# Gate and up products of a gated FFN: three partial sums kept in one PSUM bank, three VectorE additions a call in place of seven

## Chip, cores and metric
The kernel runs on one core of one Trainium2 chip. The metric is the device time of one execution in microseconds (us); lower is better. The chip multiplies on TensorE (PE), adds elementwise on VectorE (DVE) and GpSimd (POOL), applies functions and copies on ScalarE (ACT), and starts most transfers from SyncE (SP).

## What is computed
The reference is a two-layer decoder trunk on 1024 tokens of width 1024 in float32: layer 0 mixes tokens by a convolution module, layer 1 by stick-breaking attention. Both layers then do the part that the change is in:

```python
u = x @ w_up                                        # (1024, 1024) @ (1024, 2816)
g = causal_dwconv(x @ w_gate, conv_w, conv_b)       # 3 taps along the tokens
ffn = (silu(g) * u) @ w_down                        # (1024, 2816) @ (2816, 1024)
x = layer_norm(ALPHA * x + ffn + ple, ln_g, ln_b)
```

## The kernel before
Every float32 operand of a product is split into a high and a low part, and a product is three matmuls (high by high, high by low, low by high), lines 137 to 139 in `mm3`. High parts are cast on ACT, low parts are a subtraction on POOL or DVE (line 86).

`ffn_phase` (line 235) runs once in each layer. It takes the 2816 columns in steps of two tiles of 128 (`f` = 0, 2, ..., 20). A step calls `gate`, then `down` for the two tiles of the step before, then `up`. `gate` and `up` each call `fast` (line 311), so there are 11 steps by 2 calls by 2 layers, 44 calls.

A call of `fast` does a two by two block product (two halves of the contracted width, two column tiles, two halves of the tokens) by seven block products in place of eight (Winograd's form of Strassen's method). `fast_w` (line 286) loads the weights, forms their sums on DVE (line 294) and splits seven blocks on ACT (line 299) and POOL. A block product `prod(j, ps, x)` is 12 matmuls of 128x512 into one PSUM bank. The sums of the products are formed by `add` (line 322) on DVE, which reads one operand from a bank and the other from a `pt` tile in SBUF; `p1` is first copied there by ACT (line 326).

`fast` gets four banks `pa, pb, pc, pd`. There are two sets of four, used in turn by `gate`, `down` and `up`:

```python
(b0, b2), (b1, b3) = ((t[:, 0:HALF], t[:, HALF:]) for t in (big(), big()))
quads = turns(([b0, b1, b2, b3], banks))
```

So in one set `pa` and `pc` are the two halves of one tile of 1024 columns, `big0`, and `pb` and `pd` those of another, `big1`; a profile row names both `big`. In the other set each bank is a tile of its own, `bank`. By the turns, 24 of the 44 calls work in `big`: in each layer `gate` at f = 0, `gate` and `up` at f = 2, 6, 10, 14 and 18, and `up` at f = 20. The other 20 work in `bank`. `down` (line 374) works in the set that the `gate` before it did not use: it adds the product of the hidden tiles and `w_down` to the residual, 16 groups of six matmuls, each followed by an addition on DVE (line 383).

After `fast`, `gate` reads the four banks with ACT (line 348) and DVE (line 353), `up` with DVE (line 364), then ACT casts (line 366) and DVE subtracts (line 86) to get the parts of the hidden tile `f` that `down` reads.

Nothing is ordered by hand here. The library that builds the program sets the order of the instructions on each engine from their order in the source and from its own estimate of when each is ready, so matmuls of `down` and of the next call stand between the products of a call. It also places all waits.

Of the kernel before, what the change touches and what calls it, by code (L numbers as in the profile page):

```python
# [15 lines left out]
DRAM = bass.MemoryType.DRAM  # L16
# [5 lines left out]
HALF = 512  # L22
# [29 lines left out]
def trunk_kernel(ctx: ExitStack, tc, x, p, a_pw1_w, a_pw1_b, a_dw_w, a_dw_b, a_ln_g, a_ln_b, a_pw2_w, a_pw2_b,  # L52
# [37 lines left out]

    # ---------------------------------------------------------------- constants
    # one tile for all of them
    ctile = const.tile([P, 352], F32, name="ctile")
# [17 lines left out]
    class Rows:  # L111
        """Tiles of 4 KB, three to a slot."""

# [22 lines left out]
    def mm3(o, sh, sl, mh, ml, first, last):  # L136
        nc.tensor.matmul(out=o, lhsT=sh, rhs=mh, start=first, stop=False)  # L137
        nc.tensor.matmul(out=o, lhsT=sh, rhs=ml, start=False, stop=False)  # L138
        nc.tensor.matmul(out=o, lhsT=sl, rhs=mh, start=False, stop=last)  # L139

    def new_half():
        """High and low parts of a matrix (k, t) for the tokens of a half, in two tiles of four k blocks each."""
        return [[xtp.tile([P, 4, HALF], F32R, name="xT", align_bytes=A4) for _ in range(2)] for _ in range(2)]
# [20 lines left out]
    def ln_stats(src):  # L164
        nt = np_.tile([P, 24], F32, name="norm")
        st, mv, ve = nt[:, 0:12].rearrange("p (i s) -> p i s", i=2), nt[:, 12:14], nt[:, 14:16]
        rstd, tmp, nb = nt[:, 16:17], nt[:, 17:18], nt[:, 18:19]
        for i in range(2):
            nc.vector.bn_stats(out=st[:, i, :], in_=src[:, i * HALF:(i + 1) * HALF])
        nc.vector.bn_aggr(out=mv, in_=st)  # L170
        # reciprocal square root: a first guess from the exponent bits, then Newton steps to float32
        nc.vector.tensor_scalar(out=ve[:, 0:1], in0=mv[:, 1:2], scalar1=EPS, scalar2=None, op0=ALU.add)
        nc.vector.tensor_scalar(out=ve[:, 1:2], in0=mv[:, 1:2], scalar1=EPS, scalar2=-0.5, op0=ALU.add, op1=ALU.mult)
        nc.vector.tensor_scalar(out=tmp.bitcast(I32), in0=ve[:, 0:1].bitcast(I32), scalar1=1, scalar2=None,
                                op0=ALU.logical_shift_right)
        nc.vector.tensor_scalar(out=rstd.bitcast(I32), in0=tmp.bitcast(I32), scalar1=-1.0, scalar2=float(0x5f3759df),
                                op0=ALU.mult, op1=ALU.add)
        for _ in range(3):
            nc.vector.scalar_tensor_tensor(out=tmp, in0=rstd, scalar=ve[:, 1:2], in1=rstd, op0=ALU.mult, op1=ALU.mult)
            nc.vector.scalar_tensor_tensor(out=rstd, in0=tmp, scalar=1.5, in1=rstd, op0=ALU.add, op1=ALU.mult)  # L180
        return mv, rstd, nb
# [11 lines left out]

    # ---------------------------------------------------------------- p @ ple_w_proj, kept in DRAM until it is needed
    def ple_proj(i, sb, dst):
        """Pieces of work that need no result of the trunk."""
        pT, ws = [], []
# [36 lines left out]

    # ---------------------------------------------------------------- conv gated FFN + per-layer embedding
    def ffn_phase(i, xT, res, pp, g, b, sb, finish):
# [35 lines left out]

        # Gate and up projection: (W11 W21; W12 W22) of the two k halves and two column tiles, times (x11 x12; x21 x22) of
        # the two k halves and token halves, in seven block products (Strassen's, in Winograd's form).
        (x11, x21), (x12, x22) = ([[part[b] for part in xT[half]] for b in range(2)] for half in range(2))
# [10 lines left out]
        def fast_w(w, f):  # L286
# [9 lines left out]
            def split(full):  # L296
                hl = wslot(F32R).rearrange("p (o k n) -> p o k n", o=2, k=4)
                h, l = hl[:, 0], hl[:, 1]
                nc.scalar.copy(out=h, in_=full)  # L299
                sub_l(nc.gpsimd, l, full, h)  # L300
                return h, l
# [4 lines left out]
            add(s2, s1, a11, ALU.subtract)  # L306
            ws = [split(t) for t in (a11, s2, s1, a21, a12)]
            add(a12, a12, s2, ALU.subtract)
            return ws + [split(a12), split(a22)]

        def fast(w, f, quad):
            """The products of column tiles f and f + 1 with all tokens, each in two parts."""
            pa, pb, pc, pd = quad
            ws = fast_w(w, f)

            def prod(j, ps, x):
                (wh, wl), (xh, xl) = ws[j], x
                for k in range(4):
                    mm3(ps, wh[:, k, :], wl[:, k, :], xh[:, k, :], xl[:, k, :], k == 0, k == 3)

            def add(out, ps, t):
                nc.vector.tensor_tensor(out=out, in0=ps, in1=t, op=ALU.add)

            p1, u2 = parts()
            prod(0, pa, x11)
            nc.scalar.copy(out=p1, in_=pa)
            prod(1, pb, t2)
            add(u2, pb, p1)
            u5, u7 = parts()
            prod(2, pc, t1)  # L330
            add(u5, pc, u2)
            prod(3, pd, t3)
            add(u7, pd, u2)
            add(pd, pd, u5)
            prod(4, pa, x21)
            add(pa, pa, p1)
            prod(5, pb, x22)
            add(pb, pb, u5)
            prod(6, pc, t4)
            add(pc, pc, u7)  # L340
            return [[(pa, 0), (pb, HALF)], [(pc, 0), (pd, HALF)]]

# [41 lines left out]

        # two sets of four banks
        (b0, b2), (b1, b3) = ((t[:, 0:HALF], t[:, HALF:]) for t in (big(), big()))
# [18 lines left out]

    # ---------------------------------------------------------------- layer 0
    x2d_dram = dram.tile([S, D], F32, name="x2_dram")
# [4 lines left out]
    with ExitStack() as l0:  # L412
# [3 lines left out]
        with ExitStack() as ph:  # L416
# [43 lines left out]

            # pointwise 1, the gate, and the depthwise convolution as three half-rate ones of the even, the odd and
            # the summed tokens: y_even = E + O', y_odd = B - E - O with the taps of even, odd and both places
            HB = 15 + HALF
# [18 lines left out]
            def depthwise(c, hb):  # L482
                nc.vector.tensor_tensor(out=hb[:, 2, :], in0=hb[:, 0, :], in1=hb[:, 1, :], op=ALU.add)
                # both: ACT multiplies, Pool adds. Tap k of E, O and B reads 15 - k places back.
                pb = sb.tile([P, HALF], F32, name="pb", bufs=2)
# [26 lines left out]
                yv = y.rearrange("p (m a) -> p m a", a=2)  # L512
                # the bias: in B already; E + O' takes it here
                nc.vector.scalar_tensor_tensor(out=yv[:, :, 0], in0=e, scalar=vec_a[:, 16 + c:17 + c], in1=os_[:, 0:HALF],
# [104 lines left out]

    # ---------------------------------------------------------------- output projection  # L620
    res = [None] * 8
# [30 lines left out]

    # ---------------------------------------------------------------- stick breaking attention
    with ExitStack() as ph:
# [4 lines left out]
        nc.gpsimd.memset(maskb, 0.0)  # L659
        # row q, key j of the diagonal block: NEG where j >= q  # L660
        nc.gpsimd.affine_select(out=maskb, in_=maskb, pattern=[[-1, P]], compare_op=ALU.is_gt, fill=NEG,
# [13 lines left out]
        def proj_qk(w, hp, hd):  # L675
            """q: (high | low) parts over the partitions, the other way round for the odd head.
            k: high parts twice, low parts twice."""
            is_q = w is b_wq
# [25 lines left out]
        def proj_v(qt, vs):  # L704
            """Per head (high | low) parts side by side, the other way round for odd heads."""
            cs = slice(qt * 256, (qt + 1) * 256)
# [37 lines left out]
        def z_row(hd, ss, qb, a):  # L744
            """Weight of key j: sigmoid(z_j) times the product over later keys of 1 - sigmoid(z_i) = sigmoid(-z_i);
            in the last column both parts are the mask's: 0 and 1."""
            n = (qb + 1) * P
# [15 lines left out]
        def weigh(hp, half, s, i, rows, o):  # L763
            """Values weighted, for head s and the four query blocks of a half."""
            v = vs[hp][s]
# [46 lines left out]
        for piece in pieces(0):  # L812
            piece()
        # the first half's units end early: its output projection goes beside the last units of the second half
        units = [(hp, half, ss) for hp in range(HP - 2) for half, ss in ((0, (0, 1)), (1, (0,)), (1, (1,)))]
# [29 lines left out]

    # ---------------------------------------------------------------- norm, layer 1 FFN
    with ExitStack() as l1:
# [45 lines left out]
```

## Time and profile before

| | |
|---|---|
| time, median of three runs | 2754.74 us (2754.44 to 2757.61) |
| span of the profiled execution, first to last instruction | 2746.3 us |
| median time less that span | 8.4 us |
| TensorE busy | 2585.2 us, 94% of the span |
| VectorE busy | 1774.6 us, 65% |
| ScalarE busy | 1046.4 us, 38% |
| GpSimd busy | 1201.6 us, 44% |
| mean granted TensorE clock | 0.975 |

The profiled execution's own time is not listed apart from its span. The span is what the profile accounts for; a busy share is an average over the whole span. The FFN of layer 0 runs from about 530 to 1110 us, that of layer 1 from about 2030 us to the end. In a row, `out<-in` names the tiles written and read, a number in brackets is the idle time just before the instruction and who ended it.

### The profile page before, as it was taken

How to read it: one execution, taken by the hardware profiler on the slowest of the kernel's cores; microseconds unless marked ns; L12 is line 12 of the kernel's file. 1: busy time of each engine (PE TensorE's matmuls, PEld its weight loads, DVE VectorE, ACT ScalarE, POOL GpSimd, SP SyncE). 2: the span in 40 equal slices, each digit the busy share in tenths (PEclk: the TensorE clock that was granted, in tenths of full speed). 3: DMA queues.
4: the chain of work that ended last, by engine and by line, in shares of the span. 5: the costliest groups of instructions: out<-in, count | busy, mean ns of one | idle time of the engine just before them, and what ended most of it. 6: DMA issues, size and time to landing. Idle time of an engine off the chain costs nothing.

```text
span 2746.3 us, 34172 instructions
## 1 busy us (share of the span) xinstructions
PE 2585.2 (94%) x13300; PEld 2153.5 (78%) x13300; DVE 1774.6 (65%) x2785; ACT 1046.4 (38%) x1621; POOL 1201.6 (44%) x793
## 2 busy tenths in 40 slices
PE   8996998999999999999999999898899999999995
PEld 6885888988878778878777777588798787877874
DVE  4999769366565565583556665766946655656558
ACT  4556533233233232324555555642323332323231
POOL 3998236534434333412333333354653343433344
PEclk9998999999999999999999999999999999999998
DMA  4114421211111111222110101232221111211121
GB/s 149 47 47 153 163 68 62 77 47 61 47 54 58 52 52 46 69 92 68 32 50 23 45 25 38 73 125 89 70 69 62 47 60 48 62 46 46 47 77 61
DMA packets 149085, 179.12 MB, mean 65 GB/s; under 512 B 6508, under 2 KB 125756, under 8 KB 148924
## 3 DMA queue, kind: packets, MB, share of 16 engines
q1 hardware_dynamic: 144316, 168.56, 19.2%
q10 hardware_dynamic: 4608, 8.39, 0.8%
q8 instruction: 104, 1.70, 0.3%
q14 instruction: 57, 0.47, 0.1%
HBM read 151.76 MB, written 20.97 MB: 63 GB/s over the span
## 4 chain that ended last, share of the span: by engine, by line
PE 68%; DVE 18%; POOL 4%; issue 3%; ACT 3%; DMA 3%; SPq 0%; POOLq 0%; DVEq 0%; ACTq 0%
PE bank L137 13%; PE bank L138 13%; PE bank L139 12%; PE big L137 7%; PE big L139 7%; PE big L138 7%; PE big L739 3%; POOL w L86 3%; DVE bank L502 2%; DVE bank L509 2%; DVE pt L282 1%; DMA w<-in_ffn_w_up 1%; PE more L778 1%; PE more L779 1%; PE bank L773 1%
## 5 line engine op out<-in xcount | busy, mean ns | idle before, releaser
L86 POOL TENSOR_TENSOR w<-w 128x512 fp32r<-128x512 f32 (+1 forms) x444 | 755.8, 1716 | 1086.9 <-ACT w L299 675.8
L137 PE MATMUL bank<-w,xT 128*128 128x256 f32 x1280 | 367.2, 289 | 29.8 <-ACT sg L258 22.7
L299 ACT CAST w<-w 128x512 fp32r<-128x512 f32 x308 | 180.1, 619 | 542.0 <-DVE w L294 147.6
L138 PE MATMUL bank<-w,xT 128*128 128x256 f32 x1280 | 366.1, 287 | 1.4 <-POOL w L86 1.4
L139 PE MATMUL bank<-w,xT 128*128 128x256 f32 x1280 | 365.9, 288 | 0.9 <-DVE xT L86 0.9
L760 POOL TENSOR_TENSOR res<-res,rr 128x639 f32<-128x639 f32 (+3 forms) x96 | 150.2, 1565 | 316.2 <-DVE rr L758 290.0
L758 DVE TENSOR_TENSOR_SCAN rr<-rr,ctile 128x127 f32<-128x127 f32 (+7 forms) x128 | 180.1, 1428 | 162.2 <-ACT rr L756 162.1
L137 PEld LDWEIGHTS bank<-w,xT 128*128 128x128 f32 x1280 | 248.9, 195 | 32.6 <-ACT sg L258 24.1
L138 PEld LDWEIGHTS bank<-w,xT 128*128 128x128 f32 x1280 | 249.8, 195 | 2.5 <-POOL w L86 2.1
L139 PEld LDWEIGHTS bank<-w,xT 128*128 128x128 f32 x1280 | 248.5, 195 | 1.9 <-DVE xT L86 1.5
L132 ACT CAST w<-w 128x1024 fp32r<-128x1024 f32 x136 | 142.6, 1049 | 240.5 <-PE bank L138 42.8
L137 PE MATMUL big<-xT,w 128*128 128x512 f32 x544 | 212.0, 390 | 0.0
L138 PE MATMUL big<-xT,w 128*128 128x512 f32 x544 | 211.9, 389 | 0.0
L139 PE MATMUL big<-xT,w 128*128 128x512 f32 x544 | 211.6, 389 | 0.0
L137 PE MATMUL bank<-xT,w 128*128 128x512 f32 x496 | 197.4, 398 | 0.7 <-DVE m L86 0.6
L139 PE MATMUL bank<-xT,w 128*128 128x512 f32 x496 | 196.0, 395 | 0.0
L138 PE MATMUL bank<-xT,w 128*128 128x512 f32 x496 | 195.7, 394 | 0.0
L294 DVE TENSOR_TENSOR w<-w 128x512 f32<-128x512 f32 x176 | 126.9, 741 | 100.2 <-POOL w L86 50.4
L383 DVE TENSOR_TENSOR m<-m,bank 128x512 f32<-128x512 f32 x192 | 128.8, 682 | 85.0 <-PE bank L139 84.9
L137 PE MATMUL bank<-w,f 128*128 128x512 f32 x448 | 170.5, 395 | 7.7 <-ACT f L366 4.3
L138 PE MATMUL bank<-w,f 128*128 128x512 f32 x448 | 176.1, 393 | 0.0
L139 PE MATMUL bank<-w,f 128*128 128x512 f32 x448 | 173.2, 390 | 0.0
(161 smaller groups left out, 5969.4 us busy)
## 6 DMA issues: line engine op xcount, KB each, us to landing
w<-in_ffn_w_gate SPq DMA_DIRECT2D x44, 512.0 KB
w<-in_ffn_w_up SPq DMA_DIRECT2D x44, 512.0 KB
w<-in_ffn_w_down SPq DMA_DIRECT2D x44, 512.0 KB
w<-in_a_pw_w SPq DMA_DIRECT2D x32, 512.0 KB
pp<-o ACTq DMA_DIRECT2D x32, 256.0 KB
w<-in_ple_w_gate SPq DMA_DIRECT2D x16, 512.0 KB
w<-pp SPq DMA_DIRECT2D x16, 512.0 KB
w<-in_b_wo SPq DMA_DIRECT2D x16, 512.0 KB
```

The lines of the kernel that those rows point to most:

```text
L86: eng.tensor_tensor(out=l, in0=full, in1=h.bitcast(F32), op=ALU.subtract)
L132: nc.scalar.copy(out=h[:, 0:n], in_=raw)
L137: nc.tensor.matmul(out=o, lhsT=sh, rhs=mh, start=first, stop=False)
L138: nc.tensor.matmul(out=o, lhsT=sh, rhs=ml, start=False, stop=False)
L139: nc.tensor.matmul(out=o, lhsT=sl, rhs=mh, start=False, stop=last)
L294: nc.vector.tensor_tensor(out=out, in0=a, in1=c, op=op)
L299: nc.scalar.copy(out=h, in_=full)
L383: nc.vector.tensor_tensor(out=rv, in0=rv, in1=ps, op=ALU.add)
L502: nc.vector.scalar_tensor_tensor(out=e, in0=v, scalar=w, in1=e, op0=ALU.mult, op1=ALU.add)
L739: nc.tensor.matmul(out=ps[:, at + c0:at + c0 + w], lhsT=q[ks, qs], rhs=k[ks, c0:c0 + w], start=(j == 0), stop=(j == 1 and not diag))
L758: nc.vector.tensor_tensor_scan(out=rv[:, i, 1:n][:, ::-1], data0=rv[:, i, 1:n][:, ::-1], data1=zero.broadcast_to([P, n - 1]), initial=1.0, ...
L760: nc.gpsimd.tensor_tensor(out=av[:, :, 0:n - 1], in0=av[:, :, 0:n - 1], in1=rv[:, :, 1:n], op=ALU.mult)
```

## The change
The seven products and their meaning stay. Their order, their banks and the way they are summed change: product 2 is accumulated by TensorE onto product 0 in `pa`, product 4 onto that, product 6 onto that, and product 5 onto product 3 in `pc`. ACT copies `pa` after product 0 (`p1`), `pa` after product 2 (`u2`) and `pc` after product 3 (`p4`) to SBUF; DVE makes three additions. The blocks of the weights are split in the new order of their use. Comments and docstrings are also removed.

```diff
-            ws = [split(t) for t in (a11, s2, s1, a21, a12)]
+            ws = [split(t) for t in (a11, a12, s2, a21, s1, a22)]
             add(a12, a12, s2, ALU.subtract)
-            return ws + [split(a12), split(a22)]
+            return ws + [split(a12)]
...
-            def prod(j, ps, x):
+            def prod(j, ps, x, more=False):
                 (wh, wl), (xh, xl) = ws[j], x
                 for k in range(4):
-                    mm3(ps, wh[:, k, :], wl[:, k, :], xh[:, k, :], xl[:, k, :], k == 0, k == 3)
+                    for i, (s, m) in enumerate(((wh, xh), (wh, xl), (wl, xh))):
+                        nc.tensor.matmul(out=ps, lhsT=s[:, k, :], rhs=m[:, k, :], start=(k == 0 and i == 0 and not more),
+                                         stop=(k == 3 and i == 2), skip_group_check=True)
...
             p1, u2 = parts()
+            p4, _ = parts()
             prod(0, pa, x11)
             nc.scalar.copy(out=p1, in_=pa)
-            prod(1, pb, t2)
-            add(u2, pb, p1)
-            u5, u7 = parts()
-            prod(2, pc, t1)
-            add(u5, pc, u2)
-            prod(3, pd, t3)
-            add(u7, pd, u2)
-            add(pd, pd, u5)
-            prod(4, pa, x21)
-            add(pa, pa, p1)
-            prod(5, pb, x22)
-            add(pb, pb, u5)
-            prod(6, pc, t4)
-            add(pc, pc, u7)
-            return [[(pa, 0), (pb, HALF)], [(pc, 0), (pd, HALF)]]
+            prod(1, pb, x21)
+            add(pb, pb, p1)
+            prod(2, pa, t2, True)
+            nc.scalar.copy(out=u2, in_=pa)
+            prod(3, pc, t3)
+            nc.scalar.copy(out=p4, in_=pc)
+            prod(4, pa, t1, True)
+            add(pd, pa, p4)
+            prod(5, pc, t4, True)
+            add(pc, pc, u2)
+            prod(6, pa, x22, True)
+            return [[(pb, 0), (pa, HALF)], [(pc, 0), (pd, HALF)]]
```

## Rows read from the trace of the kernel before

**Rows 1.** The page's part 1: busy us, share and instructions of each engine.

```profile
PE 2585.2 (94%) x13300; PEld 2153.5 (78%) x13300; DVE 1774.6 (65%) x2785; ACT 1046.4 (38%) x1621; POOL 1201.6 (44%) x793
```

**Rows 2.** Waits of PE, whole span: total us, times, longest us.

```profile
PE big L137 <- DVE m L383: 21.6, 16, 2.9
...
PE bank L137 <- ACT f L366: 4.3, 2, 2.2
...
PE bank L137 <- DVE m L383: 3.2, 3, 1.6
...
PE big L137 <- ACT pt L326: 2.2, 10, 0.2
```

**Rows 3.** Groups by line and shape: low parts of weights, sums of weights, additions, copies.

```profile
L86 POOL TENSOR_TENSOR w<-w 128x512 fp32r<-128x512 f32 x308 | 405.6, 1337 | 698.5 <-ACT w L299 675.8 <-DVE big L322 17.1 <-DVE f L353 5.6
...
L294 DVE TENSOR_TENSOR w<-w 128x512 f32<-128x512 f32 x176 | 126.9, 741 | 100.2 <-POOL w L86 50.4 <-DMA w<-in_ffn_w_up 47.5 <-DMA w<-in_ffn_w_gate 1.5
...
L322 DVE TENSOR_TENSOR big<-big,pt 128x512 f32<-128x512 f32 x96 | 66.7, 695 | 77.5 <-PE big L139 77.5
...
L326 ACT COPY pt<-big 128x512 f32<-128x512 f32 x24 | 14.1, 586 | 27.8 <-issue 16.0 <-PE big L139 11.8
```

**Rows 4.** Timeline of PE, up call in big at f = 2: product 1's early matmuls.

```profile
603.00 0.39 PE L137 MATMUL big<-tT,w 128*128 128x512 f32 x1
...
605.04 0.39 PE L137 MATMUL big<-tT,w 128*128 128x512 f32 x1
```

**Rows 5.** Timeline of all engines, same call: end of product 0 to start of product 2.

```profile
615.92 0.39 PE L139 MATMUL big<-xT,w 128*128 128x512 f32 x1
...
616.15 0.39 PE L138 MATMUL big<-tT,w 128*128 128x512 f32 x1
...
616.35 0.59 ACT L326 COPY pt<-big 128x512 f32<-128x512 f32 x1 [0.83 <-PE big L139]
616.38 0.39 PE L139 MATMUL big<-tT,w 128*128 128x512 f32 x1
...
616.99 0.50 PE L137 MATMUL big<-tT,w 128*128 128x512 f32 x1 [0.22 <-ACT pt L326]
...
617.32 0.40 PE L138 MATMUL big<-tT,w 128*128 128x512 f32 x1
```

**Rows 6.** Timeline of PE, same call: starts of product 4, next call's product 0, product 6.

```profile
622.58 0.39 PE L137 MATMUL big<-xT,w 128*128 128x512 f32 x1
...
628.02 0.39 PE L137 MATMUL bank<-xT,w 128*128 128x512 f32 x1
...
630.74 0.39 PE L137 MATMUL big<-tT,w 128*128 128x512 f32 x1
```

**Rows 7.** Timeline of PE, gate call in big at f = 6: products 2, 3, then down's.

```profile
700.98 0.39 PE L139 MATMUL big<-tT,w 128*128 128x512 f32 x1
701.21 0.39 PE L137 MATMUL big<-tT,w 128*128 128x512 f32 x1
...
703.93 1.07 PE L137 MATMUL bank<-w,f 128*128 128x512 f32 x4
704.84 0.39 PE L137 MATMUL big<-xT,w 128*128 128x512 f32 x1
```

**Rows 8.** Timeline of all engines, gate call in bank at f = 8 with down in big.

```profile
776.89 0.68 DVE L322 TENSOR_TENSOR bank<-bank,pt 128x512 f32<-128x512 f32 x1
777.49 0.67 DVE L383 TENSOR_TENSOR m<-m,big 128x512 f32<-128x512 f32 x1
...
778.22 0.49 PE L137 MATMUL big<-w,f 128*128 128x512 f32 x1 [2.87 <-DVE m L383]
```

**Rows 9.** Windows: busy us (count) of PE, PEld, DVE, ACT, POOL; granted clock; DMA.

```profile
610.00:634.00 24.00, 23.78 (x105) 19.34 (x104) 11.18 (x18) 7.93 (x14) 13.31 (x11) 1.00 0.15 47
...
763.00:781.00 18.00, 15.13 (x63) 12.13 (x62) 14.02 (x20) 5.33 (x8) 6.06 (x4) 0.94 0.20 58
2282.00:2300.00 18.00, 17.03 (x68) 13.91 (x69) 8.90 (x15) 5.39 (x8) 3.88 (x3) 0.91 0.00 0
```

## The prediction

> **What bounds the kernel now.** The page's busy shares come first: TensorE is busy 2585.2 of 2746.3 us and no other engine passes 65% [rows 1]. The change leaves the number of matmuls alone, so it can move the time in two ways only: by adding or removing stretches in which TensorE waits, and by what such stretches do to its clock. Time taken off VectorE is worth nothing in itself. So the second view is what TensorE waits for. In the two FFN stretches the list is short: 16 + 3 waits of `down` for a residual addition on VectorE (line 383), 21.6 + 3.2 = 24.8 us; 2 waits for the cast of a hidden tile, 4.3 us; and 10 waits, all in `big`, for the copy of `p1`, counted with 2.2 us [rows 2]. The third view is the timeline of single calls, for the work that stands between a product and whoever reads its bank.
>
> The pace first. From the start of product 4 to the start of the next call's product 0, 24 matmuls later, 5.44 us pass [rows 6]: 0.227 us a matmul, 2.72 us a product, the same as in the next twelve. A call's products take 7 by 2.72 = 19 us, and nearly everything that ACT and DVE do for them fits beside that.
>
> **What the rows show of `big`.** The ten waits for `p1` are the key. In the up call at f = 2, ten of the twelve matmuls of product 1 had run early, before product 0 [rows 4]. After product 0 the remaining two run at 616.15 and 616.38, and then the first of product 2 waits until 616.99, when the copy of 616.35 to 616.94 is over [rows 5]. That copy reads `pa`; product 2 writes `pc`. They share no bank, but they are halves of one tile, `big0`. So a matmul into either half waits for a reader of the other. I take this to hold for VectorE readers too.
>
> The Trainium skill, page "PSUM — Partial Sum Buffer", section "PSUM bank collisions raise a hardware error", says that readers and writers of PSUM need guarding from each other by bank, which would let product 2 go on here. The wait in the trace is therefore not asked for by the chip's banks but placed by the tile; by the page's rule alone the sum below would lose all its costs, which is the first rival.
>
> **The change part by part.**
>
> *Work removed and added.* 4 of 7 additions go from each of 44 calls: 176 by 0.695 us [rows 3] = 122 us off VectorE. Two copies come to each call: 88 by 0.586 us [rows 3] = 52 us onto ACT, which is busy 7.93 of 24 us in an up call in `big` and VectorE 11.18 [rows 9]. Both lie beside TensorE. What counts is who waits for them.
>
> *New hand-overs, `bank` set (20 calls).* Product 2 into `pa` waits for copy `p1`, with product 1 between; product 4 waits for copy `u2`, with product 3 between; product 5 into `pc` waits for `p4`, with product 4 between; product 6 waits for the addition into `pd`, with product 5 between. Each has 2.72 us of cover against 0.59 or 0.69 us of work. I cost them at nothing. Where the reader is held up in its queue by over 2 us, or the product between has run early, a hand-over costs up to the price below.
>
> *New hand-overs, `big` set (24 calls).* Products 2, 3, 4, 5 and 6 now all write halves of `big0`, and between each two of them somebody reads a half of it: copy `u2` after product 2, copy `p4` after 3, the addition into `pd` after 4, that into `pc` after 5. By the rule read above each is a wait with no product of this call between; before, neighbouring products alternated between `big0` and `big1`. The price of one without cover is read from the `p1` wait [rows 5]: product 0's last matmul starts at 615.92, the next could start at 616.15; with nothing to put there TensorE would resume at 616.99, 0.84 us later, and the second start follows after 0.33 instead of 0.23. That is 0.94 us after a copy. After an addition (0.695 for 0.586) it is 1.05 us. Queued work on ACT or DVE comes on top.
>
> What stands ready to fill these places: in a gate call `down`'s matmuls of the step before, as four of them already do between products 3 and 4 [rows 7]; in an up call nothing of `down` is left, and the next call's product 0 serves, which now runs before product 6 [rows 6]. When its weights come early enough for the place after product 2 the trace doesn't show, since no place was open there. Bounds for all 96 hand-overs: 0 if everything is filled, 48 by 0.94 + 48 by 1.05 = 95 us if nothing is. My sum:
> - up calls at f = 2 to 18, ten: the `p1` wait grows from 0.49 (0.39 + 0.10) to at most 0.94 when all of product 1 runs early, +0.45; after product 2 the full 0.94; after 3 half of 0.94, as the next product 0 is partly ready; after 4 and 5 filled. 1.86 by 10 = 19 us.
> - gate calls at f = 0, two, where no `down` exists: 0.94 + 0.94 = 1.9 by 2 = 4 us.
> - gate calls at f = 2 to 18, ten: filled by `down`; 0.3 each for places it doesn't fill, as between products 2 and 3, where no other matmul stands now [rows 7]: 3 us.
> - up calls at f = 20, two: the last `down` fills with the older hidden pair: 0.
> - queue delay, some 0.15 us for 25 open places: 4 us.
>
> Together +30 us.
>
> *What VectorE gives back.* In the step shown `down`'s third group waits until 778.22 for an addition of 777.49, which queues right behind the 0.68 us addition into `pc` [rows 8]. That addition is no longer behind product 6 but behind product 5, and `pb` is done after product 1. If each of the 19 waits shrinks by one addition: 13 us at most. The waits end on the tail of `gate`'s reads of its banks, which now come after product 6 into `pa` instead of `pc`, so I take half, 6.5 us. Where a wait was near 3 us the granted clock of that stretch is 0.94 or 0.91 [rows 9], between the two levels of 1.2 and 2.4 GHz: 18 by 0.06 = 1.1 and 18 by 0.09 = 1.6 us; for four such stretches 5 us, of which I take 4. The last product of a call needs no addition after it: 0.695 us at the end of each layer's last up call, 1.4 us. Together -12 us; bounds 0 and -25 (13 + 5 + 1.4 and the rest of the 24.8).
>
> *Order of the weight splits.* Product 1 now uses a block that needs no sum on VectorE, and product 6 the one with two sums, one place later than before. Product 0 and the products ahead hide it; with the cover gone it is one POOL subtraction, 1.34 us [rows 3], for a call. SP issues the same loads. Cost 0. Unused `pt` halves: the same two tiles a call, 0.
>
> **Sum:** +30 - 12 = +18 us on a span of 2746.3, so 2764; the median of the runs lies 8.4 us above that span: 2773 us. One part in 500, 5.5 us, is what I treat as the least that a measurement can tell.
>
> **Rivals.**
> 1. *Faster: the hand-overs are filled.* The library fills every open place by its own estimates, or the tile rule doesn't reach the new pairs. For: in the gate call fillers stand exactly where products waited [rows 7], and the ten `p1` waits are the only ones of this kind in 44 calls. Against: the up calls have only one product in store, and the `p1` waits were not filled. Then only the gain is left, 2755 - 12 = 2743, with all of it 2730. It decides if an up call has a spare product ready from product 2 on. Chance 0.24.
> 2. *Slower still: nothing fills.* The next call's weights come late, since slots come free no earlier, and every place of `big` stands open with queueing: 95 - 12 = +83, 2838 us. Against: rows 6 show a product ready in reserve. Chance 0.12.
> 3. *Even:* places after products 3 to 5 are filled, half of those after 2, gain in full: +14 - 14, 2755 us. Chance 0.16.
> 4. *The additions don't go:* excluded by the source, three `add` calls remain; below 0.01.
>
> **How the numbers follow.** Forecast +18, 0.48, its own range 2762 to 2795. Slower by over 0.2%: 0.48 + 0.12 = 0.60. Within: 0.16. Faster: 0.24. The range takes in most of the fast case and the bounds of the forecast, not the far end of rival 2: 2737 to 2815.
>
> **What would show it.** TensorE's waits should list `big` waiting for line 326 copies (over 20 times, 0.5 us or more each) and for `pd` or `pc` additions, while `bank` lists hardly any; line 322 should count 132, copies 132; VectorE some 1655 us, ACT some 1100. `down`'s waits should fall below 20 us and the four clock dips shrink. Wrong if `big` shows no such waits, or `bank` shows as many as `big`: then the tile is not the cause.

## The result, and the profile after

The changed kernel is slower, and by more than was forecast: 2800.84 us median of four runs (2798.45 to 2805.1), beside 2754.59 us for the kernel before in the same job. The ratio is 1.017 [1.0155, 1.0185], +46 us where the sum gave +18. The sign held; the sum did not, and the profile shows that its two terms were off in opposite directions.

The page's part 1 of the changed kernel (busy us, share and instructions of each engine), under its span:

```profile
span 2796.6 us, 34046 instructions
...
PE 2603.1 (93%) x13300; PEld 2155.9 (77%) x13300; DVE 1657.3 (59%) x2609; ACT 1089.6 (39%) x1709; POOL 1196.3 (43%) x793
```

Beside [rows 1], VectorE went from 1774.6 to 1657.3 us and ACT from 1046.4 to 1089.6, close to the 1655 and 1100 announced. TensorE's idle time, span less busy, went from 161.1 to 193.5 us, +32.4. Its busy time for the same 13300 matmuls rose by 17.9 us; the mean granted clock fell from 0.975 to 0.969, and 2796.6 by 0.031 is 87 us of lost clock where 2746.3 by 0.025 was 69: the same +18. (All four executions of the changed kernel have 0.967 to 0.969; the 17 of the kernel before in e1's job have a median of 0.972.) Together that is +50.3 us of span. It is 4 us more than the difference of the medians, because the span before lies 8.4 us below its median and the span after 4.2.

The tile view counts 72 additions in `big` and 60 in `bank`, 132, with medians of 700 ns, and as many copies, of 584 to 589 ns in `big`; both were forecast so.

Below is what TensorE waits for in the changed kernel (total us, times, longest us). Line numbers have shifted: matmuls of products 321, additions 325, copies 330 (`p1`), 334 (`u2`) and 336 (`p4`), taps of `gate` 354, `down`'s addition 384.

```profile
PE big L137 <- DVE m L384: 25.2, 8, 3.2
...
PE big L139 <- DVE f L86: 11.0, 14, 1.3
...
PE big L321 <- DVE f L354: 7.2, 6, 2.5
PE big L321 <- ACT pt L330: 6.8, 10, 0.7
...
PE big L321 <- DVE big L325: 3.3, 4, 0.8
...
PE big L321 <- DVE m L384: 2.1, 8, 0.4
```

These six lines hold 55.6 us, where `big` had 21.6 + 2.2 = 23.8 in [rows 2]: +31.8, so nearly the whole +32.4 of idle time is in them. The hand-overs between products make 6.8 + 3.3 = 10.1 us, 7.9 more than before. Most of the rest is at `down`: the waits for its residual addition and for the low part of the hidden tile are 25.2 + 11.0 + 2.1 = 38.3 us, 16.7 more, where the prediction had them shrink. The remaining 7.2 us are the first products of the calls at f = 2, waiting for the taps of the `gate` call before them on the same tiles.

How that comes about is seen in one up call, the one of [rows 4 to 6], `big` at f = 2. TensorE's timeline of the changed kernel, like instructions in one row:

```profile
615.67 5.69 PE L321 MATMUL big<-xT,w 128*128 128x512 f32 x24 [2.48 <-DVE f L354]
622.04 3.02 PE L321 MATMUL big<-tT,w 128*128 128x512 f32 x12 [0.68 <-ACT pt L330]
624.89 2.88 PE L321 MATMUL bank<-xT,w 128*128 128x512 f32 x12
627.61 2.88 PE L321 MATMUL big<-tT,w 128*128 128x512 f32 x12
630.33 2.88 PE L321 MATMUL bank<-xT,w 128*128 128x512 f32 x12
633.05 2.88 PE L321 MATMUL big<-tT,w 128*128 128x512 f32 x12
635.77 5.38 PE L321 MATMUL bank<-tT,w 128*128 128x512 f32 x23
640.99 2.88 PE L321 MATMUL big<-tT,w 128*128 128x512 f32 x12
643.71 3.11 PE L321 MATMUL bank<-tT,w 128*128 128x512 f32 x13
646.65 2.88 PE L321 MATMUL big<-xT,w 128*128 128x512 f32 x12
649.37 2.88 PE L321 MATMUL bank<-tT,w 128*128 128x512 f32 x12
652.09 2.88 PE L321 MATMUL bank<-xT,w 128*128 128x512 f32 x12
654.81 0.39 PE L137 MATMUL big<-w,f 128*128 128x512 f32 x1
```

One place stays open, after product 0 and 1 (0.68 us). Each later place, between products 2, 3, 4, 5 and 6, is filled with products of the next `gate` call, in `bank`: five of its seven have run when up's product 6 starts at 646.65. So the end of `up` moves late (before, product 6 stood at 630.74, [rows 6]), and only two `bank` products are left between it and `down`, which needs up's result. In the kernel before there were six, 633.46 to 649.78 by 2.72 us each:

```profile
633.46 0.39 PE L137 MATMUL bank<-tT,w 128*128 128x512 f32 x1
...
649.78 0.39 PE L137 MATMUL big<-w,f 128*128 128x512 f32 x1
...
654.14 0.50 PE L137 MATMUL big<-w,f 128*128 128x512 f32 x1 [1.48 <-DVE m L383]
```

VectorE's timeline of the changed kernel from there on, with the two waits of TensorE that follow:

```profile
649.57 1.29 DVE L365 TENSOR_TENSOR f<-f,big 128x512 f32<-128x512 f32 x2 [1.95 <-PE big L321]
...
654.68 0.69 DVE L294 TENSOR_TENSOR w<-w 128x512 f32<-128x512 f32 x1 [3.82 <-DMA w<-in_ffn_w_up]
655.29 1.22 DVE L86 TENSOR_TENSOR f<-f 128x1024 fp32r<-128x1024 f32 x1
...
658.23 1.22 DVE L86 TENSOR_TENSOR f<-f 128x1024 fp32r<-128x1024 f32 x1
659.36 3.37 DVE L354 SCALAR_TENSOR_TENSOR f<-bank,ctile,f 128x511 f32<-128x511 f32 x5
662.65 1.27 DVE L384 TENSOR_TENSOR m<-m,big 128x512 f32<-128x512 f32 x2
```

```profile
659.50 0.73 PE L139 MATMUL big<-w,f 128*128 128x512 f32 x2 [1.27 <-DVE f L86]
663.39 0.80 PE L137 MATMUL big<-w,f 128*128 128x512 f32 x1 [3.15 <-DVE m L384]
```

The ends of `up` and `gate` now meet. `down` begins at 654.81, the low parts it reads come at 655.29 and 658.23, the first behind a weight sum that held the queue for 3.82 us until its transfer arrived, the second behind more sums and an addition; the five taps on `gate`'s banks stand ahead of `down`'s first addition. Windows of the changed kernel over the same place (busy us of PE, PEld, DVE, ACT, POOL, then granted clock, DMA share, GB/s):

```profile
656.00:659.00 3.00, 1.66 (x6) 1.05 (x6) 3.00 (x5) 1.25 (x2) 0.00 (x0) 1.00 0.01 3
659.00:662.00 3.00, 0.73 (x2) 0.30 (x2) 3.00 (x6) 0.71 (x2) 1.27 (x1) 0.98 0.00 0
662.00:664.00 2.00, 0.61 (x2) 0.52 (x3) 2.00 (x5) 0.00 (x0) 0.00 (x0) 0.50 0.00 0
664.00:668.00 4.00, 4.00 (x11) 3.13 (x10) 3.10 (x5) 2.11 (x2) 0.00 (x0) 0.50 0.00 0
```

VectorE is busy without a break to 664 while TensorE works 3.0 of 8 us. From 662 to 668 the granted clock is 0.50, the lower of its two levels (1.2 of 2.4 GHz): in the last 4 us stand 11 matmuls, where 17.6 fit at the 0.227 us of [rows 6].

### The profile page after: what moved, and what is told of

It is laid out like the page before. It is cut to its first block, busy times and chain, and to the rows that moved or that the text cites. A ratio compares the mean times of both kernels' runs of the same rounds, so it can differ in the third digit from the quotient of the medians.

```text
span 2796.6 us, 34046 instructions
## 1 busy us (share of the span) xinstructions
PE 2603.1 (93%) x13300; PEld 2155.9 (77%) x13300; DVE 1657.3 (59%) x2609; ACT 1089.6 (39%) x1709; POOL 1196.3 (43%) x793
## 5 line engine op out<-in xcount | busy, mean ns | idle before, releaser
L321 PE MATMUL big<-tT,w 128*128 128x512 f32 x1152 | 279.3, 391 | 8.5 <-ACT pt L330 6.8
L321 PEld LDWEIGHTS big<-tT,w 128*128 128x128 f32 x1152 | 214.4, 188 | 60.3 <-ACT pt L330 11.8
L321 PE MATMUL bank<-tT,w 128*128 128x512 f32 x960 | 227.3, 389 | 0.0
L321 PE MATMUL big<-xT,w 128*128 128x512 f32 x864 | 207.2, 391 | 10.8 <-DVE f L354 7.2
L321 PEld LDWEIGHTS bank<-tT,w 128*128 128x128 f32 x960 | 180.2, 188 | 37.4
L325 DVE TENSOR_TENSOR big<-big,pt 128x512 f32<-128x512 f32 x72 | 50.3, 698 | 258.4 <-PE big L321 187.2
L321 PEld LDWEIGHTS big<-xT,w 128*128 128x128 f32 x864 | 160.8, 188 | 50.1 <-issue 7.9
L294 DVE TENSOR_TENSOR w<-w 128x512 f32<-128x512 f32 x176 | 140.7, 816 | 91.3 <-DMA w<-in_ffn_w_up 36.6
L321 PE MATMUL bank<-xT,w 128*128 128x512 f32 x720 | 178.1, 392 | 0.6 <-ACT w L299 0.6
L138 PE MATMUL bank<-w,f 128*128 128x512 f32 x448 | 174.4, 389 | 0.0
L139 PE MATMUL bank<-w,f 128*128 128x512 f32 x448 | 173.4, 389 | 0.0
```

The lines of the kernel that those rows point to most:

```text
L294: nc.vector.tensor_tensor(out=out, in0=a, in1=c, op=op)
L321: nc.tensor.matmul(out=ps, lhsT=s[:, k, :], rhs=m[:, k, :], start=(k == 0 and i == 0 and not more), stop=(k == 3 and i == 2), skip_group_c ...
```

## Experiments

Theory A, the prediction's: products that share a tile make hand-overs, and these are what the change costs. The trace of the result adds to it that they cost through what fills them. The rivals: the new order of the weight splits, VectorE's queue, and the moved additions by themselves. Each ratio is to the kernel before in the same job; idle time is TensorE's, span less busy, of the profiled run (161.1 before, 193.5 changed).

| run | median us | ratio to before | idle us | busy us |
|---|---|---|---|---|
| the changed kernel | 2800.84 | 1.017 [1.0155, 1.0185] | 193.5 | 2603.1 |
| e1_swap_halves | 2739.26 | 0.9937 [0.992, 0.9954] | 156.6 | 2579.3 |
| e3_before_shared | 2760.28 | 1.002 [1.0008, 1.0031] | 170.5 | 2584.9 |
| e4_gate_behind | 2787.54 | 1.0114 [1.0099, 1.0129] | 188.4 | 2596.5 |
| e7_old_split_order | 2784.89 | 1.0115 [1.0099, 1.0131] | 179.2 | 2602.7 |
| e5_sums_on_pool | 2766.47 | 1.0041 [1.0025, 1.0057] | 176.0 | 2587.7 |
| e9_before_pool | 2716.53 | 0.9865 [0.9849, 0.9881] | 141.7 | 2571.4 |
| e6_swap_and_pool | 2721.44 | 0.9884 [0.9868, 0.99] | 140.7 | 2576.7 |
| e8_swap_dve_work | 2755.30 | 1.0011 [1.0002, 1.0021] | 167.7 | 2584.0 |
| e10_swap_less_work | 2751.65 | 0.9989 [0.998, 0.9998] | 162.2 | 2585.6 |

**e1_swap_halves: is it the tile?** The changed kernel with the roles of two banks exchanged. The banks, the work and its order in the source stay; in `big`, `pa` now shares a tile with `pd` and no longer with `pc`.

```diff
-            pa, pb, pc, pd = quad
+            pa, pb, pd, pc = quad
```

> The changed kernel with one line different: in the call pc and pd change places, so that pa and pd are the halves of one tile and pb and pc of the other; consecutive products then write different tiles. Theory A, shared tile: the open places between products go, the next gate call's products are no longer pulled ahead of the up call's last one, and the time falls from 2801 to 2735 to 2758 us; waits of big for copies (lines 330 to 336) under 1 us in all, waits of big for line 384 from 25 back to under 16 us. Rival B, the accumulation itself (more ACT copies, a longer chain through one bank): stays at 2785 to 2801. Rival C, the new order of the weight splits: 2775 or more, with the long waits of down still there.

2739.26 us: 61 us off the changed kernel, and 17 below the kernel before. Here are TensorE's waits in this run, the ones that answer to the list above and one that is new, and three of its products 2 to 5 in the call shown above:

```profile
PE bank L321 <- DVE bank L325: 10.8, 7, 2.8
...
PE big L321 <- ACT pt L330: 3.4, 10, 0.3
...
PE big L137 <- DVE m L384: 1.5, 8, 0.2
```

```profile
618.43 8.48 PE L321 MATMUL big<-tT,w 128*128 128x512 f32 x36 [0.34 <-ACT pt L330]
```

The three products run without a break and nothing is put between them. `down`'s waits in `big` fall from 25.2 to 1.5 us, and the low parts leave the list. The copies still hold 3.4 us, where under 1 was expected. So the whole loss hangs on which two banks are halves of one tile. What is new is a wait in `bank`, seven times, for an addition. In the step shown above it is `gate`'s product 6, which waits until 654.20 for the addition that reads its own bank; the addition stood behind three weight sums, and the first of these waited 3.24 us for a transfer. It is a hand-over that the prediction costed at nothing, on the condition that no queue holds its reader for over 2 us. e1 is ahead of the kernel before in spite of it.

**e3_before_shared: the same exchange without the change.** The kernel before with the same exchange. Its product 1 goes to `pb` and product 2 to what is now the other half of the same tile, so that more neighbours in the source share.

```diff
-            pa, pb, pc, pd = quad
+            pa, pb, pd, pc = quad
```

> The kernel before with the same swap of pc and pd: now products 1 and 2, 3 and 4, 5 and 6 write the two halves of one tile with a reader between. Theory A: fillers are pulled forward in the up calls or places stay open, slower than before by 10 to 45 us (2765 to 2800). Rival B (only the accumulation matters): 2750 to 2760.

2760.28 us, +3.5 to the before of its job: a miss, below what theory A expected and at the upper end of what its rival did. The waits of this run show a hand-over of the new kind, ten of 0.8 us, while `down`'s stay nearly as they were:

```profile
PE big L137 <- DVE m L383: 23.5, 8, 3.2
...
PE big L137 <- DVE pt L322: 7.7, 10, 0.9
```

These waits don't show that shared neighbours are cheap, for most of the sharing was not met. In the up call at f = 6 the products 1 to 3 run without a break, 36 matmuls from 737.62 on, and the second of the three starts at 740.34, before the addition that reads product 1's bank:

```profile
740.34 0.39 PE L137 MATMUL big<-tT,w 128*128 128x512 f32 x1
...
740.61 0.69 DVE L322 TENSOR_TENSOR pt<-big,pt 128x512 f32<-128x512 f32 x1 [2.56 <-PE big L139]
```

By the rule of the tile it can't be product 2, which writes the other half of that bank's tile. So the library took product 3 ahead of it, and these neighbours write different tiles again. (The rows don't number the products; the order is inferred.) The changed kernel leaves no such order: products 2, 4 and 6 add up in one half of a tile and 3 and 5 in the other. e1 and e3 ran in one job and have the same halves, so their difference is what the change gives where few neighbours share: 21 us less, with `down`'s addition in `big` at 1.5 us in place of 23.5.

**e4_gate_behind: open places without fillers.** The changed kernel with every matmul of a `gate` call held, by the library's means, until product 6 of the `up` call before it. The places in `up` then stay open.

```diff
+                behind = w is ffn_w_gate and ends
+                with tc.issue_after(ends[-1]) if behind else ExitStack():
...
+                if j == 6 and w is ffn_w_up:
+                    ends.append(mm.ins if hasattr(mm, "ins") else mm)
```

> The changed kernel with the products of a gate call held behind product 6 of the up call before it on TensorE's queue, nothing else. Theory T1, the time was lost because fillers brought the end of up and the end of gate together ahead of down: the waits of big for line 384 and for the low parts (36 us together) fall to under 16 us and the clock rises to 0.973, while the four hand-overs of ten up calls now stand open, 10 by 3.6 = 36 us, in waits for lines 330, 334, 336 and 325; time 2785 to 2805. Rival T2, the hand-overs are cheap or hidden in other ways: 2760 or less. Rival T3, down's waits have nothing to do with the order of products but with VectorE's queue being held by a transfer: they stay at 30 us or more and the time rises to about 2835.

2787.54 us, 13 us faster than with the fillers, as theory T1 expected. Its waits follow (lines shifted again: copies 336, 340, 342, additions 331, `down`'s addition 390):

```profile
PE big L325 <- DVE big L331: 19.8, 24, 0.9
...
PE big L325 <- ACT pt L342: 6.8, 10, 0.7
PE big L325 <- ACT pt L340: 6.8, 10, 0.7
PE big L325 <- ACT pt L336: 6.8, 10, 0.7
...
PE big L137 <- DVE m L390: 2.8, 9, 0.7
```

Here are the hand-overs of the prediction, one by one: 30 behind copies at 0.68 us and 24 behind additions at 0.825 us of idle time. A matmul lasts 0.39 and the next could start after 0.227, so the delay is 0.16 more: 0.84 and 0.98 us, beside the 0.84 and, with 0.695 for 0.586, the 0.95 worked out from [rows 5]. With the slower starts behind it a copy costs 0.98 (products start at 623.77 and 627.47, less 2.72) and an addition 1.09 to 1.16, where the prediction took 0.94 and 1.05. The waits come to 40.2 us of idle time. And `down`'s waits for its addition, 25.2 us in the changed kernel, are 2.8, and those for the low parts are off the list. The fillers saved 30 us of open places and cost more than that at `down` (36 us) and in TensorE's busy time (7 us, by the clock).

**e7_old_split_order: is it the splits?** The changed kernel with the blocks of the weights split in the old order.

```diff
-            ws = [split(t) for t in (a11, a12, s2, a21, s1, a22)]
+            h11, h2, h1, h21, h12 = [split(t) for t in (a11, s2, s1, a21, a12)]
             add(a12, a12, s2, ALU.subtract)
-            return ws + [split(a12)]
+            h4, h22 = split(a12), split(a22)
+            return [h11, h12, h2, h21, h1, h22, h4]
```

> The changed kernel with the weight blocks split in the order of the kernel before. Product 1's block then comes fifth, so the next call has fewer products ready when places open. Theory T1 (fillers pulled forward): the order of products changes and with it down's waits; they fall if the next gate call ends later, 2780 to 2800, or the open places cost more, up to 2815. Rival C (the new split order made the loss): back under 2765.

2784.89 us, 32 us above the before of its job: some 14 of the 46 us go, but 32 stay. The wait of `down` hardly moves (its addition is line 385 here):

```profile
PE big L137 <- DVE m L385: 24.5, 8, 3.1
```

The order of the splits is thus a part, not the cause. 14 us of idle time went: the low parts (11.0) and the waits of products for `down`'s addition (2.1) are no longer on the list, and the waits for the taps are 2.5 shorter.

**e5_sums_on_pool: VectorE's queue.** The changed kernel with the weight sums of line 294 on GpSimd, so that no wait for a transfer stands in VectorE's queue.

```diff
-                nc.vector.tensor_tensor(out=out, in0=a, in1=c, op=op)
+                nc.gpsimd.tensor_tensor(out=out, in0=a, in1=c, op=op)
```

> The changed kernel with the four sums of weight blocks a call (line 294) on GpSimd instead of VectorE; the order of products on TensorE is nearly the same. Theory T3, the low part of the hidden tile stands on VectorE behind a weight sum that waits for its transfer (3.8 us at 651 to 655): without it the waits for the low part (11 us) go, the wait for line 384 falls from 3.2 to under 2 us each, the clock dips vanish: 2755 to 2772. Theory T1 alone (two ends of calls in one place, whatever holds VectorE): the wait for line 384 stays at 2.5 us or more each, time 2785 to 2800. GpSimd's queue could make weights late: then new waits of big or bank at line 321 for GpSimd.

2766.47 us, 34 us off the changed kernel: within what theory T3 expected, below what T1 alone did. Its waits:

```profile
PE big L137 <- DVE m L384: 12.8, 8, 2.3
PE bank L137 <- ACT w L132: 12.2, 7, 2.0
...
PE big L321 <- ACT pt L330: 6.8, 10, 0.7
```

In the call shown above, TensorE's order is nearly that of the changed kernel (two `bank` products between `up` and `down`), but over the whole span `down`'s waits for its addition are half as long, and those for the low parts are off the list. A new wait, for the casts of `down`'s weights on ACT (line 132), gives 12.2 us of it back.

**e9_before_pool and e6_swap_and_pool: is that gain the change's?** The same edit of line 294 in the kernel before, and in e1.

> The kernel before with the four sums of weight blocks a call on GpSimd. If VectorE's queue held by a weight sum that waits for its transfer is also behind down's waits there (24.8 us, clock dips of some 5 us): 2728 to 2742, waits of big for line 383 under 12 us. Rival: down's waits come from the amount of additions at the call's end: 2748 to 2758.

> The kernel of e1_swap_halves with the four sums of weight blocks a call on GpSimd. What is left there of waits in the FFN is 10.8 us of product 6 in bank for line 325 and 3.4 us for the first copy; if VectorE's queue being held by a weight sum that waits for its transfer (theory T3) is behind the first, those 10.8 us go: 2722 to 2734, unless weights come late from GpSimd (waits of line 137 for the cast at line 132 were 12 us in e5), then 2735 to 2745. Rival: the wait is the length of the chain through pa itself: unchanged, about 2739.

2716.53 and 2721.44 us. The first lies below the range expected of it; it is the fastest kernel of all, and holds nothing of the change. The second is 18 us below e1, and the seven waits in `bank` are gone. Against e5, with the sums on GpSimd in both, the change still costs 0.0176 of the time, some 48 us: relief of VectorE speeds both kernels alike and leaves the cost of the change where it was. By the pairs with and without the sharing, the changed kernel against e1 and e5 against e6, the sharing itself costs some 64 us without this relief and 43 with it. In e9's waits `down`'s additions in `big` are gone from the list, and the copies of `p1` are what remains in `big`:

```profile
PE big L137 <- ACT pt L326: 6.3, 10, 0.7
```

The 176 sums take 1307 ns each on GpSimd and 741 on VectorE [rows 3], and the kernel is faster all the same. The edit takes two things off VectorE, 127 us of work and the 100.2 us for which its queue stood still ahead of a sum [rows 3]; which of them gives more was not separated. Between e6 and e9 the intervals overlap: with VectorE relieved in this way, the change brings nothing that these runs can tell, even without the sharing.

**e8_swap_dve_work and e10_swap_less_work: what is e1's gain?** e1 with four, and with two, additions of SBUF tiles a call put back on VectorE, into an unused half tile that nothing reads; this work enters no result.

```diff
+            nc.vector.tensor_tensor(out=spare, in0=p1, in1=p1, op=ALU.add)
```

> The kernel of e1_swap_halves with four additions from SBUF to SBUF put back onto VectorE in each call (into an unused half of a pt tile; they add to no result). Theory D (the gain of e1 over the kernel before, 17 us, is VectorE's relief): most of it goes, 2748 to 2758, and down's waits for line 384 come back to 15 us or more. Rival (the gain is the shape of the call's end: no addition after product 6, three banks done early): stays at 2735 to 2744.

> The kernel of e1_swap_halves with two additions from SBUF to SBUF a call put onto VectorE, near the work of the four additions that the change removed (a SBUF addition took longer than one from PSUM in e8). Theory D (the gain of e1 is the relief of VectorE): between, 2744 to 2756. Rival (e8 lost by the long additions standing ahead of single sums): 2735 to 2744.

2755.30 and 2751.65 us. With work back on VectorE e1's gain is nearly or wholly gone. But it does not go the way it came. In e8 the waits are

```profile
PE bank L321 <- DVE bank L325: 12.4, 7, 3.4
PE big L321 <- DVE big L325: 12.0, 10, 1.5
...
PE big L137 <- DVE m L388: 1.5, 8, 0.2
```

with `down`'s still short, where 15 us or more were expected, and ten new ones between products. The dose is not the removed one either: an SBUF addition takes longer than one from a bank (last section), and VectorE was busy 1909.4 us here and 1803.0 in e10, where e1 has 1699.9 and the kernel before 1774.6. So these runs agree with a gain by relief of VectorE, but don't show it. What they do show is that `down`'s wait in `big` is 1.5 to 1.7 us in all four runs without the sharing (e1, e6, e8, e10), whatever work VectorE has, beside 21.6 before and 23.5 in e3. That fall comes with the changed order, even where VectorE has more work than in the kernel before (e8, e10); whether it is the earlier place of the additions, as the prediction argued, or the place of `down` among the next products was not separated. The old order loses these waits too, in e9, once the sums are out of VectorE's queue.

## Why the prediction was right and wrong

**Right.** The rule read from [rows 5] holds, that a matmul into one half of a tile waits for a reader of the other half, and that VectorE's reads count too: e1 exchanges two names and takes 61 us off, and e4 has 24 waits behind additions. The price of one open place was nearly right, 0.94 us behind a copy and 1.05 behind an addition, where e4 shows 0.98 and 1.09 to 1.16. The counts and the busy times of VectorE and ACT came as forecast. The `bank` set, whose banks are tiles of their own, lists no hand-overs in the changed kernel. By the Trainium skill's page "PSUM — Partial Sum Buffer", section "PSUM bank collisions raise a hardware error", guarding is needed by bank. Here the waits were placed by tile, and without sharing (e1) the time is 2739 us, near the 2743 of the first rival. The closeness is in part luck: in e1 `down`'s waits in `big` fall by 20.1 us where the rival counted 6.5 for all of `down`'s, and 10.8 us are new in `bank`.

**Off in size: the term of the hand-overs, +30 us.** The step "in an up call nothing of `down` is left, and the next call's product 0 serves" left some of the places after products 2 and 3 open. In the trace these places are filled, the next `gate` call having not one but five products to give: no wait for `u2` or `p4` stands in the list, and waits for copies came to ten, not over twenty. Measured were +7.9 us, and 7.2 more for first products behind the taps; in the call shown product 1 no longer ran ahead of product 0 as in [rows 4]. So the term was 15 us and not 30.

**Wrong: the term "What VectorE gives back", -12 us.** It let `down`'s waits shrink by an addition each and the clock dips with them. `down`'s waits rose by 16.7 us instead, and the clock cost 18 us, so the term was +35. The fault lies in the step before it: a filled place was costed at nothing. Filling is a change of order. What was moved ahead (`gate`'s products) had until then stood between `up` and `down` and covered `up`'s tail on VectorE; taken from there, it left `down` waiting for low parts, taps and additions in one queue. The prediction named the cover of each hand-over, but not what that cover had been covering. In e4, which gives the cover back, `down`'s wait is 2.8 us, and in e1, where no place has to be filled, it is 1.5: the shrinking that the prediction forecast does come, once the sharing is gone. A slip that moved nothing in the forecast: the bound -25, added up as written (13 + 5 + 1.4 and the rest of the 24.8), is -31, and with it the 2730 of the first rival is 2724; the even case takes the full gain at 14 where the parts named make 19.

**The rivals.** The first ("the hand-overs are filled") had its mechanism nearly right and its sign wrong: the places were filled, and this made the kernel slower than open places would have. The second, nothing filled at +83, was not run in full; in e4, with the places of the `up` calls open, the time is 31 us above the before of that job. The even case fell with the same step as the forecast.

**What stays open.** Between e5 and e9 lie 34 us of idle time and 16 of busy time. The waits add up to the idle time (in e5 12.8 + 12.2 us at `down`, 13.2 at hand-overs and 2.6 behind taps, in e9 6.3 for `p1`), but no run takes them apart. So the cost of the sharing with VectorE relieved (43 us) is measured, but its path is not shown. Each half of `big` as a tile of its own wasn't tried either; e1 takes away the sharing that the change's neighbours make, not all of it.

## What to carry to other kernels

Before putting partial sums into fewer banks, list for each pair of neighbouring products which tile they write and who reads it in between: in this program a wait went by the tile, and two banks in one tile counted as one. Look too whether the order leaves another product to put between them. Where such a place can be filled, ask what the filler covered where it stood; here the gaps filled with the next call's products brought the tails of two calls together ahead of the step that needed the first. And look at what is queued ahead of the work that others wait for: weight sums moved off VectorE to an engine that takes 1.8 times as long for them gave 38 us, more than the change with other halves (17).

## What the runs showed of the hardware that was not expected

- Additions with both operands in SBUF took longer than the ones removed, which read one from a bank. In e8 the four lines of 128x512 SBUF additions have medians of 0.69, 0.91, 1.36 and 1.78 us, single ones up to 2.88, where those that read a bank stay between 0.681 and 0.700. The timeline of e8 shows what stood beside them, one with nothing on GpSimd and one beside a subtraction there:

```profile
582.32 0.68 DVE L337 TENSOR_TENSOR pt<-pt 128x512 f32<-128x512 f32 x1
...
584.06 2.88 DVE L340 TENSOR_TENSOR pt<-pt 128x512 f32<-128x512 f32 x1
```

```profile
583.26 3.12 POOL L86 TENSOR_TENSOR w<-w 128x1024 fp32r<-128x1024 f32 x1 [2.55 <-ACT w L132]
```

The one that ran from 584.06 to 586.94 lies beside GpSimd's, 583.26 to 586.38, which itself took 3.12 us for a group mean of 2.47 in the changed kernel. The Trainium skill's page "GPSIMD Engine Reference", section "1. Specifications", says that GpSimd shares its SBUF interface with VectorE and contends with instructions of two SBUF inputs there. These rows agree, though no run here takes the one away to see the other alone. The weight sums, two SBUF operands each, point the same way: the same 176 took 741 ns on average before, 816 in the changed kernel and 946 in e1. So VectorE's busy time is not the count of its instructions times a fixed cost: e1 has as many as the changed kernel and is busy 43 us longer. GpSimd was busy 1227.7 us in e8 and 1219.9 in e10, beside 1207.2 in e1, another way in which the work put back is not the dose that was removed.
- Many short waits cost little clock in e4: it has 54 of 0.7 to 0.9 us, and its mean clock is 0.974 (0.026 of 2784.9 us lost, 72 us, beside 69 before). The changed kernel has fewer but longer ones, up to 3.15 us and close together; in the call shown 6 us at 0.50 follow, and over the span 87 us are lost.
